# Opening of a two-layer decoder trunk: shift and scale columns of a chunk in one tile, TensorE in the first steps, even rates for the later vectors

## The chip, the cores and the metric

The kernel runs on one core of a Trainium2 chip. The metric is the device time of one execution in microseconds (us), lower is better; the time of a kernel is the median of its runs.

The engines that matter are TensorE (PE: matmuls and transposes; PEld: its weight loads), VectorE (DVE), ScalarE (ACT), GpSimd (POOL) and SyncE (SP), which issues most of the transfers. Each engine works through its own list of instructions in order; they wait for each other on semaphores.

## The reference

One sequence of 256 tokens, width 2048, goes through two layers. Each has a token mixer (layer 0: forgetting attention, `fox`; layer 1: sliding-window attention, `swa`) and a gated feed-forward block with a short convolution. Each of the four sub-layers is modulated by vectors that come from one conditioning vector `c`:

```python
c_act = silu(c)                                    # (1, 2048)
for i in range(2):
    mod = c_act @ ada_w[i] + ada_b[i]              # ada_w[i]: 2048 x 12288, float32
    sh1, sc1, g1, sh2, sc2, g2 = split(mod, 6)
    h = x * (1 + sc1) + sh1
    y = fox_attention(h, ...) if i == 0 else swa_attention(h, positions, ...)
    x = layer_norm(ALPHA * x + (1 + g1) * y, ln_mix_g[i], ln_mix_b[i])
    h = x * (1 + sc2) + sh2
    y = conv_ffn(h, ...)
    x = layer_norm(ALPHA * x + (1 + g2) * y, ln_ffn_g[i], ln_ffn_b[i])
```

All is float32. A vector (`sh1` and so on) is the product of a row of 2048 with a 2048 x 2048 block of `ada_w`, 16.8 MB that are read once.

## The kernel before

**Weights.** A weight tile is 256 rows by 512 columns (`[128, 2, 512]`, 512 KB). `stream` issues its transfer on SP, ACT copies it to the rounded half `wh`, DVE subtracts to get the low half `wl`, and PE multiplies with three products of halves: 24 matmuls of 256 columns where the weights are stationary (`w_mm`, results `ws`), 12 of 512 columns where the activations are (`x_mm`, results `xs`). The activations are kept as halves `hH`, `hL`, transposed, in 16 row chunks of 128. The pool `wp` has ten tile buffers for all tiles that SP loads, `hl` four pairs of halves. A planner in the framework orders the instructions of each engine; instructions given to `pin` keep their place in the program.

**Vectors.** `ada_vector(l, v)` makes vector v of layer l. It reads `ada_w` in 32 tiles (`wa`), and DVE adds each, scaled by an element of `cact`, to an accumulator `acc` of 128 x 2048 whose partitions still have to be summed. For a gate (v 2 and 5, a row) PE sums with `onep`. For a column vector four groups of four PE transposes of `acc` are summed by ACT, and `finish` makes the columns `cv`. A vector in `HELD`, (0,4) and (1,4), is not summed there: its PE sums (`sums`, 16 matmuls with `ones`) are kept in `held` until `release`, which `between` calls in the layer norm that needs it, and no later vector starts before. Each tile of weights that PE has used is a tick (`ada_tick`): it adds `ada["rate"]` to a debt, and each whole unit of it is one step of the running vector (usually one `wa` tile and one DVE product). `ada_need` runs steps until a vector is there.

**Opening.** The first products need the shift and scale of layer 0, v 0 and 1. `opening` makes them in five stages of 2, 2, 4, 4 and 4 column chunks (`widths`). In a stage `sums` loads the tiles of the shift and then those of the scale (`wo`); DVE does 14 of the 16 row chunks of each, PE chunks 7 and 15, as products with one column (`cps`). Then PE adds DVE's accumulator `oacc` with `ones`, DVE adds the bias (`cv`), and `mod_turn` (transposes of x) and `mod_pair` give the chunks of `hH` and `hL`. While a stage's vectors come in, PE works on weight tiles of the attention's input projection for the chunks that the earlier stages made (`plan`: 0, 3, 9, 12 and 12 tiles in the five stages, 6 more behind them).

**Later.** Then blocks 1, 2 and 3 of the projection (54 tiles) with the attention heads in between, `out_proj` (32 tiles, four quarters of the columns, the first two together), the layer norm with `between`, and the feed-forward block. The rates of the ticks are 0 in the opening, then 1.2 to 1.4, and in `out_proj` 1.4, 1.4 and 1.8 in the last two quarters.

**Layer norm.** `residual` adds the gated result to x, 512 columns at a time, and gathers statistics on DVE; POOL makes 1/sqrt (`rs`), `normalise` scales the first half of the tokens on ACT and the second on DVE, and `modulate` transposes, shifts and scales for the next sub-layer. `fox` clears `fh` and `fl`, the halves of the forget weights, with POOL.

Of the kernel before, what the change touches and what calls it, by code (L numbers as in the profile page):

```python
# [41 lines left out]
def hybrid_trunk(ctx: ExitStack, tc: tile.TileContext, a: dict, out: bass.AP):  # L42
# [31 lines left out]
    def mm(o, lhsT, rhs, start=False, stop=False, **kw):  # L74
        return nc.tensor.matmul(o, lhsT, rhs, start=start, stop=stop, **kw)  # L75
# [11 lines left out]
    def split_v(h, l, src):  # L87
        nc.vector.tensor_copy(h, src)
        nc.vector.tensor_tensor(l, src, f32(h), op=ALU.subtract)


    rows0 = ttile("rows0").rearrange("p (a b) -> p a b", b=P)
# [3 lines left out]
    nc.sync.dma_start(rows0[:NADA, 1, :], adab[0])  # L96

    ident = cst.tile([P, P], F32, name="ident")
    nc.gpsimd.memset(ident, 0.0)
    nc.gpsimd.affine_select(out=ident, in_=ident, compare_op=ALU.not_equal, fill=1.0, base=0,  # L100
                            pattern=[[-1, P]], channel_multiplier=1)
    ones = cst.tile([P, P], F32, name="ones")
    nc.gpsimd.memset(ones, 1.0)
    onep = cst.tile([P, P], F32, name="onep")
# [27 lines left out]
    nc.tensor.transpose(pt[:, :NADA], rows0[:NADA, 1, :], ident[:NADA, :NADA])  # L132
    nc.vector.tensor_copy(acol[:, 0, :], pt[:, :NADA])

    NF = 2 * DFF // P
# [228 lines left out]
    gates = {}  # L364
    ada_list = [(0, 2), (0, 3), (0, 4), (0, 5), (1, 0), (1, 1), (1, 3), (1, 2), (1, 4), (1, 5)]
    ada = {"gen": None, "debt": 0.0, "rate": 0.0, "gate_free": True}

    held = []
    HELD = {(0,4):False,(1,4):False}

# [144 lines left out]
    def opening(plan, proj, prep):  # L515
# [5 lines left out]

        def sums(c0, CB, v, acc, ps):
            QK = 1024 // CB
            nb = CB // P
            for kq in range(0, KC, QK):
                w = wp.tile([P, QK, CB], F32, tag="w", name="wo")
                nc.sync.dma_start(w, a["ada_w"][0, kq * P:(kq + QK) * P, v * D + c0:v * D + c0 + CB]
                                  .rearrange("(k p) f -> p k f", p=P))
                for k in range(QK):
                    kc = kq + k  # L530
                    if kc % 8 >= 8 - 1:
                        for j in range(nb):
                            c = nb * v + j
                            mm(ps[:, c:c + 1], w[:, k, j * P:(j + 1) * P], cact[:, kc:kc + 1],
                               start=c == 0 and kc == 8 - 1, skip_group_check=True)
                    elif kc == 0:
                        nc.vector.tensor_scalar_mul(acc[:, v, :], w[:, k, :], cact[:, kc:kc + 1])
                    else:
                        nc.vector.scalar_tensor_tensor(acc[:, v, :], w[:, k, :], cact[:, kc:kc + 1],
                                                       acc[:, v, :], op0=ALU.mult, op1=ALU.add)  # L540
                yield
# [3 lines left out]
        for s_, items in enumerate(plan):  # L545
            todo = [(*it, part) for it in items for part in range(3)]
            n = len(todo)
            if s_ == len(widths):
                for it in todo:
                    proj(*it)  # L550
                break
# [4 lines left out]
            ps = bank("cps")  # L556
            steps = [g for v in range(2) for g in [sums(c0, CB, v, acc, ps)] * (KC * CB // 1024)]
            for i, g in enumerate(steps):
# [6 lines left out]
            if s_ == 1:  # L565
                prep()
            for c in range(2 * nb):
                mm(ps[:, c:c + 1], acc[:, c // nb, c % nb * P:(c % nb + 1) * P], ones[:, 0:1],
                   stop=True, skip_group_check=True)
            for k in range(k0, k0 + nb, 2):  # L570
                tps = mod_turn(k)
                if k == k0:
                    for v in range(2):
                        nc.vector.scalar_tensor_tensor(cols[0, v][:, k:k + nb], ps[:, nb * v:nb * (v + 1)], float(v),
                                                       acol[:, 0, v * KC + k:v * KC + k + nb],
                                                       op0=ALU.add, op1=ALU.add)
                mod_pair(cols[0, 1], cols[0, 0], k, tps)

# [123 lines left out]
    def out_proj(oT, full, w_o, l):  # L702
# [11 lines left out]
        for i, ks in enumerate((range(0, 8), range(8, 12))):  # L714
            then(lambda i=i: ada.update(rate=((1.4,1.4,1.8,1.8), (0.85,)*4)[l][i]))
            for d in range(2):
                part(d, list(ks))
        then(lambda: ada_need(l, 2))
        for d in range(D // WB):
            if d < 2:  # L720
                part(d, list(range(12, KC)))
            else:
                then(lambda d=d: ada.update(rate=((1.4,1.4,1.8,1.8), (0.85,)*4)[l][d]))
                ps[d] = x_banks()
                part(d, list(range(KC)))
            then(lambda d=d: defer(residual(ps[d], d, gates[l, 2], True)), d == D // WB - 1)
# [3 lines left out]
    def fox(l, j):  # L730
# [7 lines left out]
        for q in range(4):  # L738
            nc.gpsimd.memset(f32(fh[q]), 0.0)
            nc.gpsimd.memset(f32(fl[q]), 0.0)  # L740

# [148 lines left out]
        later([forget(), columns(), rotary(), scaled()])  # L890
        for blk, rate in zip((0, 1, 2, 3), (1.2, 1.2, 1.3, 1.4)):
            then(lambda rate=rate: ada.update(rate=rate))
# [249 lines left out]
```

## Time and profile before

| | |
|---|---|
| median of 3 runs | 2278.0 us (2277.01 to 2279.0) |
| profiled execution | 2279.87 us, its span 2278.0 us |
| mean granted clock of TensorE | 0.985 |
| busy: PE, DVE, ACT, POOL | 2217.5, 1800.6, 1159.0, 26.6 us |
| read from memory | 598.37 MB, 264 GB/s over the span |

The profile is that of one execution. A row of a timeline has the start, the time, the engine, the line, the operation, what it writes and reads with their shapes, the count (x), and in brackets the idle time of the engine before it with what ended it. A row of a table by stretches has the stretch, its length, the busy time of PE, PE's weight loads, DVE, ACT and POOL (with counts), the granted clock as a share of full speed, the share of the transfer engines and GB/s. A row of waits says who waited for whom, the microseconds in total, how often, and the longest.

### The profile page before, as it was taken

To read this page: it belongs to the slowest core of one execution; us is meant where nothing else is said; L and a number is where in the kernel's file an instruction comes from. 1 tells how busy PE (TensorE), PEld (TensorE's weight loads), DVE (VectorE), ACT (ScalarE), POOL (GpSimd) and SP (SyncE) were. 2 spreads that over 40 slices of the span, in tenths; PEclk is the share of its full clock that TensorE was granted. 3 is DMA by queue.
4 is the path that set the end of the run, shared out by engine and by line. 5 is a ranking of instruction groups with operands and counts; after the bars stand their busy time and mean duration, and the time that the engine had idled before them with its cause. 6 is when DMAs were issued, how large, how long until landed. Compare 5 with 4: busy or idle time off the path is not lost. (4 is left out here: it accounts for less than half of the span.)

```text
span 2278.0 us, 38425 instructions
## 1 busy us (share of the span) xinstructions
PE 2217.5 (97%) x14933; PEld 2037.1 (89%) x14933; DVE 1800.6 (79%) x2509; ACT 1159.0 (51%) x1821; POOL 26.6 (1%) x61
## 2 busy tenths in 40 slices
PE   5999999999999999999999999999999999999997
PEld 5899998789999988999987788789999988999986
DVE  7877988979969978789788888779878555566656
ACT  2435565445555543555644588745555533454532
POOL 1001000000000000000000000000000000000000
PEclk8999999989999999999999999999999999999999
DMA  9998989879978989889888676658878556666563
GB/s 335 340 337 278 351 303 373 310 268 318 326 257 303 309 274 350 277 277 312 276 303 299 222 268 215 215 181 291 264 259 267 185 193 193 188 189 191 186 194 111
DMA packets 273720, 603.01 MB, mean 265 GB/s; under 512 B 20790, under 2 KB 29176, under 8 KB 273024
## 3 DMA queue, kind: packets, MB, share of 16 engines
q1 hardware_dynamic: 272480, 595.85, 77.1%
q0 software_dynamic: 1056, 4.69, 0.6%
q8 instruction: 117, 1.92, 0.3%
q14 instruction: 67, 0.55, 0.1%
HBM read 598.37 MB, written 2.10 MB: 264 GB/s over the span
## 5 line engine op out<-in xcount | busy, mean ns | idle before, releaser
L266 ACT CAST wh<-w 128x1024 fp32r<-128x1024 f32 x728 | 764.4, 1052 | 860.6 <-PE ws L75 319.9
L277 DVE TENSOR_TENSOR wl<-w,wh 128x1024 fp32r<-128x1024 f32 x728 | 888.9, 1222 | 376.4 <-ACT wh L266 358.0
L75 PE MATMUL ws<-hH,wh 128*128 128x256 f32 x3328 | 937.7, 282 | 10.5 <-ACT wh L266 10.5
L75 PE MATMUL ws<-hH,wl 128*128 128x256 f32 x3328 | 930.0, 281 | 4.3 <-DVE wl L277 4.3
L75 PE MATMUL ws<-hL,wh 128*128 128x256 f32 x3328 | 933.3, 281 | 0.2 <-DVE hL L85 0.2
L75 PEld LDWEIGHTS ws<-hH,wh 128*128 128x128 f32 x3328 | 629.9, 189 | 15.1 <-ACT wh L266 11.5
L75 PEld LDWEIGHTS ws<-hH,wl 128*128 128x128 f32 x3328 | 628.1, 189 | 5.4 <-DVE wl L277 5.2
L75 PEld LDWEIGHTS ws<-hL,wh 128*128 128x128 f32 x3328 | 630.4, 189 | 2.8 <-issue 1.9
L75 PE MATMUL xs<-wh,gT 128*128 128x512 f32 x1408 | 435.5, 389 | 0.0
L75 PEld LDWEIGHTS xs<-wh,gT 128*128 128x128 f32 x1408 | 264.3, 188 | 54.8
L75 PE MATMUL xs<-wl,gT 128*128 128x512 f32 x704 | 273.9, 389 | 0.0
L395 DVE SCALAR_TENSOR_TENSOR acc<-wa,cact,acc 128x1024 f32<-128x1024 f32 x180 | 228.4, 1278 | 0.0
L395 DVE SCALAR_TENSOR_TENSOR acc<-wa,cactp,acc 128x1024 f32<-128x1024 f32 x128 | 162.7, 1279 | 0.0
L75 PEld LDWEIGHTS xs<-wl,gT 128*128 128x128 f32 x704 | 132.2, 188 | 27.2
L75 PE MATMUL xs<-wh,hH 128*128 128x512 f32 x352 | 143.6, 414 | 0.3 <-ACT hH L492 0.3
L75 PE MATMUL xs<-wl,hH 128*128 128x512 f32 x352 | 141.7, 403 | 0.0
L75 PE MATMUL xs<-wh,hL 128*128 128x512 f32 x352 | 139.8, 400 | 0.0
L75 PE MATMUL xs<-wh,oT 128*128 128x512 f32 x384 | 127.7, 402 | 0.9 <-ACT pT L687 0.8
L1029 ACT ACTIVATE u<-ws,ccol 128x256 f32<-128x256 f32 x176 | 96.6, 561 | 56.4 <-PE ws L75 47.0
L1030 DVE SCALAR_TENSOR_TENSOR u<-ws,ccol,u 128x255 f32<-128x255 f32 x176 | 82.7, 478 | 19.9 <-ACT u L1029 19.8
L75 PEld LDWEIGHTS xs<-wh,oT 128*128 128x128 f32 x384 | 73.5, 192 | 16.4 <-ACT pT L687 1.2
L1032 DVE SCALAR_TENSOR_TENSOR u<-ws,ccol,u 128x254 f32<-128x254 f32 x176 | 83.4, 478 | 2.1
(219 smaller groups left out, 1615.1 us busy)
## 6 DMA issues: line engine op xcount, KB each, us to landing
w<-in_ffn_w_up_dram SPq DMA_DIRECT2D x352, 512.0 KB, 4.7
wa<-in_ada_w_dram SPq DMA_DIRECT2D x320, 512.0 KB, 5.5
w<-in_ffn_w_down_dram SPq DMA_DIRECT2D x176, 512.0 KB, 4.8
w<-in_fox_w_in_dram SPq DMA_DIRECT2D x96, 512.0 KB, 6.5
wo<-in_ada_w_dram SPq DMA_DIRECT2D x64, 512.0 KB, 8.7
w<-in_swa_w_in_dram SPq DMA_DIRECT2D x40, 512.0 KB, 5.1
w<-in_fox_w_o_dram SPq DMA_DIRECT2D x32, 512.0 KB, 7.0
w<-in_swa_w_o_dram SPq DMA_DIRECT2D x32, 512.0 KB, 4.9
```

The lines of the kernel that those rows point to most:

```text
L75: return nc.tensor.matmul(o, lhsT, rhs, start=start, stop=stop, **kw)
L266: pin(nc.scalar.copy(h, w), False)
L277: pin(nc.vector.tensor_tensor(l, w, f32(h), op=ALU.subtract), behind[0] > 0)
L395: pin(nc.vector.scalar_tensor_tensor(ac, wo, (cactp if row else cact)[:, k:k + 1], ac, op0=ALU.mult, op1=ALU.add), True)
L1029: nc.scalar.activation(u, pf, AF.Identity, bias=cw(CW, f), scale=cw(2, f))
L1030: nc.vector.scalar_tensor_tensor(u[:, 1:], pf[:, :S - 1], cw(1, f), u[:, 1:], op0=ALU.mult, op1=ALU.add)
L1032: nc.vector.scalar_tensor_tensor(u[:, 2:], pf[:, :S - 2], cw(0, f), u[:, 2:], op0=ALU.mult, op1=ALU.add)
```

## The change

- `opening` loads shift and scale columns of a chunk together: one tile has two row chunks (stages 0 and 1) or one (the others), and both vectors' columns beside each other, `[128, QK, 2, CB]`; each row chunk is a transfer of its own. So DVE's step covers both vectors. Per stage, 16 steps less those that PE does.
- PE does the odd row chunks in stage 0, chunks 3, 7, 11 and 15 in stage 1, and chunk 15 alone in the others (`onpe`). The totals of DVE's accumulator stand ahead of the last chunk's products.
- `busy(n)` runs n float32 matmuls of `ones` with `ones` that nobody reads: 4 and 5 at the start, 3 behind each of PE's row chunks in stage 0.
- The first stage's transposes go to two banks and its modulation uses the form that writes `hH` straight from ACT.
- `HELD` is empty: (0,4) and (1,4) are summed by transposes and ACT like the others, and later vectors may start at once.
- The first two vectors change places. The rate is 1.32 from the opening's last weight tiles through all of layer 0's attention, 0.6 in the last quarter of `out_proj`; in layer 1 the last quarter has 0.3 instead of 0.85.
- `fh` and `fl` are cleared by ACT instead of POOL; `ones` is filled ahead of `ident`.

```diff
@@ -88,6 +88,12 @@
         nc.vector.tensor_copy(h, src)
         nc.vector.tensor_tensor(l, src, f32(h), op=ALU.subtract)
 
+    def busy(n):
+
+        o = bank("idle")
+        for _ in range(n):
+            mm(o[:, :P], ones, ones, start=True, stop=True)
+
 
     rows0 = ttile("rows0").rearrange("p (a b) -> p a b", b=P)
     NADA = 6 * KC
@@ -95,12 +101,13 @@
     adab = a["ada_b"].rearrange("l (r p) -> l r p", p=P)
     nc.sync.dma_start(rows0[:NADA, 1, :], adab[0])
 
+    ones = cst.tile([P, P], F32, name="ones")
+    nc.gpsimd.memset(ones, 1.0)
+    busy(4)
     ident = cst.tile([P, P], F32, name="ident")
     nc.gpsimd.memset(ident, 0.0)
     nc.gpsimd.affine_select(out=ident, in_=ident, compare_op=ALU.not_equal, fill=1.0, base=0,
                             pattern=[[-1, P]], channel_multiplier=1)
-    ones = cst.tile([P, P], F32, name="ones")
-    nc.gpsimd.memset(ones, 1.0)
     onep = cst.tile([P, P], F32, name="onep")
     nc.gpsimd.memset(onep, 1.0 / P)
 
@@ -131,6 +138,7 @@
     pt = bank()
     nc.tensor.transpose(pt[:, :NADA], rows0[:NADA, 1, :], ident[:NADA, :NADA])
     nc.vector.tensor_copy(acol[:, 0, :], pt[:, :NADA])
+    busy(5)
 
     NF = 2 * DFF // P
     HR = ROPE_DIM // 2
@@ -362,11 +370,11 @@
 
     cols = {}
     gates = {}
-    ada_list = [(0, 2), (0, 3), (0, 4), (0, 5), (1, 0), (1, 1), (1, 3), (1, 2), (1, 4), (1, 5)]
+    ada_list = [(0, 3), (0, 2), (0, 4), (0, 5), (1, 0), (1, 1), (1, 3), (1, 2), (1, 4), (1, 5)]
     ada = {"gen": None, "debt": 0.0, "rate": 0.0, "gate_free": True}
 
     held = []
-    HELD = {(0,4):False,(1,4):False}
+    HELD = {}
 
     def ada_vector(l, v):
         row = v % 3 == 2
@@ -519,25 +527,43 @@
         for v in range(2):
             cols[0, v] = cst.tile([P, KC], F32, tag=f"cv{v}", name="cv")
 
-        def sums(c0, CB, v, acc, ps):
-            QK = 1024 // CB
+
+        onpe = [range(1, KC, 2), range(3, KC, 4)] + [(KC - 1,)] * 3
+
+        def products(w, c0, CB, kc, ps, first):
             nb = CB // P
+            for c in range(2 * nb):
+                mm(ps[:, c:c + 1], w[:, c // nb, c % nb * P:(c % nb + 1) * P], cact[:, kc:kc + 1],
+                   start=c == 0 and first, stop=kc == KC - 1, skip_group_check=True)
+
+        def totals(CB, acc, ps, first):
+            nb = CB // P
+            for c in range(2 * nb):
+                mm(ps[:, c:c + 1], acc[:, c // nb, c % nb * P:(c % nb + 1) * P], ones[:, 0:1],
+                   start=c == 0 and first, skip_group_check=True)
+
+        def sums(s_, c0, CB, acc, ps):
+            QK = 512 // CB
+            pe = onpe[s_]
             for kq in range(0, KC, QK):
-                w = wp.tile([P, QK, CB], F32, tag="w", name="wo")
-                nc.sync.dma_start(w, a["ada_w"][0, kq * P:(kq + QK) * P, v * D + c0:v * D + c0 + CB]
-                                  .rearrange("(k p) f -> p k f", p=P))
+                w = wp.tile([P, QK, 2, CB], F32, tag="w", name="wo")
+                for k in range(QK):
+                    nc.sync.dma_start(w[:, k], a["ada_w"][0, (kq + k) * P:(kq + k + 1) * P, :2 * D]
+                                      .rearrange("p (v f) -> p v f", f=D)[:, :, c0:c0 + CB])
                 for k in range(QK):
                     kc = kq + k
-                    if kc % 8 >= 8 - 1:
-                        for j in range(nb):
-                            c = nb * v + j
-                            mm(ps[:, c:c + 1], w[:, k, j * P:(j + 1) * P], cact[:, kc:kc + 1],
-                               start=c == 0 and kc == 8 - 1, skip_group_check=True)
-                    elif kc == 0:
-                        nc.vector.tensor_scalar_mul(acc[:, v, :], w[:, k, :], cact[:, kc:kc + 1])
-                    else:
-                        nc.vector.scalar_tensor_tensor(acc[:, v, :], w[:, k, :], cact[:, kc:kc + 1],
-                                                       acc[:, v, :], op0=ALU.mult, op1=ALU.add)
+                    if kc not in pe:
+                        if kc == 0:
+                            nc.vector.tensor_scalar_mul(acc, w[:, k], cact[:, kc:kc + 1])
+                        else:
+                            nc.vector.scalar_tensor_tensor(acc, w[:, k], cact[:, kc:kc + 1], acc,
+                                                           op0=ALU.mult, op1=ALU.add)
+                        continue
+                    if kc == KC - 1:
+                        totals(CB, acc, ps, len(pe) == 1)
+                    products(w[:, k], c0, CB, kc, ps, kc == pe[0] and len(pe) > 1)
+                    if s_ == 0:
+                        busy(3)
                 yield
 
         accs = cst.tile([P, D], F32, tag="acc", name="oacc").rearrange("p (c v f) -> p c v f", c=2, v=2)
@@ -546,6 +572,7 @@
             todo = [(*it, part) for it in items for part in range(3)]
             n = len(todo)
             if s_ == len(widths):
+                then(lambda: ada.update(rate=1.32))
                 for it in todo:
                     proj(*it)
                 break
@@ -554,7 +581,7 @@
             pair += widths[s_]
             acc = accs[:, s_ % 2, :, :CB]
             ps = bank("cps")
-            steps = [g for v in range(2) for g in [sums(c0, CB, v, acc, ps)] * (KC * CB // 1024)]
+            steps = [sums(s_, c0, CB, acc, ps)] * (KC * CB // 512)
             for i, g in enumerate(steps):
                 if i == len(steps) // 2 and c0 % 512 == 0:
                     c = slice(c0, c0 + 512)
@@ -564,17 +591,14 @@
                     proj(*todo.pop(0))
             if s_ == 1:
                 prep()
-            for c in range(2 * nb):
-                mm(ps[:, c:c + 1], acc[:, c // nb, c % nb * P:(c % nb + 1) * P], ones[:, 0:1],
-                   stop=True, skip_group_check=True)
             for k in range(k0, k0 + nb, 2):
-                tps = mod_turn(k)
+                tps = mod_turn(k, 2 if k == 0 else 1)
                 if k == k0:
                     for v in range(2):
                         nc.vector.scalar_tensor_tensor(cols[0, v][:, k:k + nb], ps[:, nb * v:nb * (v + 1)], float(v),
                                                        acol[:, 0, v * KC + k:v * KC + k + nb],
                                                        op0=ALU.add, op1=ALU.add)
-                mod_pair(cols[0, 1], cols[0, 0], k, tps)
+                mod_pair(cols[0, 1], cols[0, 0], k, tps, k == 0)
 
 
     stats = cst.tile([P, NT, D // 512, nc.vector.BN_STATS_DIM], F32, name="stats")
@@ -712,7 +736,7 @@
             stream(w_o, 0, d * WB, ks, use)
 
         for i, ks in enumerate((range(0, 8), range(8, 12))):
-            then(lambda i=i: ada.update(rate=((1.4,1.4,1.8,1.8), (0.85,)*4)[l][i]))
+            then(lambda i=i: ada.update(rate=((1.32, 1.32, 1.32, 0.6), (0.85, 0.85, 0.85, 0.3))[l][i]))
             for d in range(2):
                 part(d, list(ks))
         then(lambda: ada_need(l, 2))
@@ -720,7 +744,7 @@
             if d < 2:
                 part(d, list(range(12, KC)))
             else:
-                then(lambda d=d: ada.update(rate=((1.4,1.4,1.8,1.8), (0.85,)*4)[l][d]))
+                then(lambda d=d: ada.update(rate=((1.32, 1.32, 1.32, 0.6), (0.85, 0.85, 0.85, 0.3))[l][d]))
                 ps[d] = x_banks()
                 part(d, list(range(KC)))
             then(lambda d=d: defer(residual(ps[d], d, gates[l, 2], True)), d == D // WB - 1)
@@ -736,8 +760,8 @@
         fh, fl = ([gtile(n).rearrange("p a b -> p (a b)").rearrange("p (k f) -> p k f", f=P) for _ in range(4)]
                   for n in ("fh", "fl"))
         for q in range(4):
-            nc.gpsimd.memset(f32(fh[q]), 0.0)
-            nc.gpsimd.memset(f32(fl[q]), 0.0)
+            for f in (fh[q], fl[q]):
+                nc.scalar.mul(f, ones.rearrange("p (o f) -> p o f", o=1).broadcast_to([P, 4, P]), 0.0)
 
         def prep():
             for b in range(4):
@@ -888,7 +912,7 @@
         opening(plan, first_block, prep)
         settle()
         later([forget(), columns(), rotary(), scaled()])
-        for blk, rate in zip((0, 1, 2, 3), (1.2, 1.2, 1.3, 1.4)):
+        for blk, rate in zip((0, 1, 2, 3), (1.32,) * 4):
             then(lambda rate=rate: ada.update(rate=rate))
             q, k, V = [], [], []
             n = done.get(blk, 0)
```

## The prediction

> **What bounds the kernel now.** I read the page first, then the busy time by stretches of 57 us, then TensorE's waits, then the timelines of the two places where they fall.
>
> ```profile
> span 2278.0 us, 38425 instructions
> ...
> PE 2217.5 (97%) x14933; PEld 2037.1 (89%) x14933; DVE 1800.6 (79%) x2509; ACT 1159.0 (51%) x1821; POOL 26.6 (1%) x61
> ```
>
> TensorE (PE) is the bound: 2278.0 - 2217.5 leaves 60.5 us idle. Its work on the weights is not touched by the change. What can be won is idle time and time at half clock; both lie in few places:
>
> ```profile
> 0.00:57.00 57.00, 32.57 (x164) 29.70 (x164) 43.17 (x88) 12.95 (x19) 8.06 (x30) 0.88 1.03 335
> 57.00:114.00 57.00, 52.73 (x350) 48.56 (x349) 46.30 (x60) 24.23 (x32) 0.00 (x0) 0.92 0.97 340
> ...
> 399.00:456.00 57.00, 53.18 (x237) 43.09 (x236) 52.93 (x69) 24.34 (x45) 0.00 (x0) 0.94 0.89 311
> 456.00:513.00 57.00, 52.41 (x284) 45.88 (x284) 45.49 (x64) 24.70 (x31) 1.74 (x3) 0.88 0.72 265
> ```
>
> The columns are length, busy time of PE, its weight loads, DVE, ACT and POOL, granted clock, DMA share, GB/s. The first two rows (the opening) lack 28.7 us of PE, the last two (out-projection of layer 0 and the layer norm behind it) 8.4 us, and the clock is below 1 in all four. Who is late:
>
> ```profile
> PE cps L75 <- DMA wo<-in_ada_w_dram: 10.9, 5, 3.6
> PE ws L75 <- ACT wh L266: 10.5, 4, 3.9
> PE xs L75 <- DVE wl L277: 7.2, 3, 3.5
> PE ws L75 <- DVE wl L277: 4.3, 4, 2.5
> ```
>
> The first, second and fourth are the opening, the third is the out-projection. In the opening VectorE (DVE) and the transfers press together, and PE's clock falls when it waits; in the out-projection DVE is alone. The four rows are the stretches that the sums below use:
>
> ```profile
> 10.00:20.00 10.00, 4.94 (x20) 4.28 (x20) 8.42 (x22) 0.00 (x0) 0.00 (x0) 1.00 1.08 349
> ...
> 40.00:50.00 10.00, 5.29 (x20) 4.71 (x21) 9.79 (x17) 3.19 (x6) 0.00 (x0) 0.50 1.04 384
> ...
> 450.00:460.00 10.00, 9.94 (x31) 7.93 (x32) 10.00 (x10) 3.15 (x3) 0.00 (x0) 0.69 1.00 378
> ...
> 470.00:480.00 10.00, 6.98 (x24) 5.59 (x25) 8.20 (x8) 2.85 (x4) 0.00 (x0) 0.83 1.05 389
> ```
>
> **The opening, DVE's and PE's work.** The five ends of stages in the old kernel are the `cv` rows; the first two rows below price DVE's product steps:
>
> ```profile
> 23.44 0.23 DVE L574 SCALAR_TENSOR_TENSOR cv<-cps,acol 128x2 f32<-128x2 f32 x2 [0.71 <-PE cps L75]
> ...
> 28.65 4.29 DVE L539 SCALAR_TENSOR_TENSOR oacc<-wo,cact,oacc 128x256 f32<-128x256 f32 x10
> ...
> 38.65 0.22 DVE L574 SCALAR_TENSOR_TENSOR cv<-cps,acol 128x2 f32<-128x2 f32 x2
> ...
> 49.17 3.10 DVE L539 SCALAR_TENSOR_TENSOR oacc<-wo,cact,oacc 128x512 f32<-128x512 f32 x4
> ...
> 81.56 0.23 DVE L574 SCALAR_TENSOR_TENSOR cv<-cps,acol 128x4 f32<-128x4 f32 x2 [1.94 <-PE cps L75]
> ...
> 128.49 0.23 DVE L574 SCALAR_TENSOR_TENSOR cv<-cps,acol 128x4 f32<-128x4 f32 x2 [5.96 <-PE cps L75]
> ...
> 171.03 0.23 DVE L574 SCALAR_TENSOR_TENSOR cv<-cps,acol 128x4 f32<-128x4 f32 x2 [4.82 <-PE cps L75]
> ```
>
> A 256-wide step costs 0.43 us, a 512-wide one 0.78. For a 1024-wide one, and for DVE's low half of a weight tile (`wl`), the out-projection has rows, beside the longest wait there:
>
> ```profile
> 444.01 4.85 DVE L395 SCALAR_TENSOR_TENSOR acc<-wa,cact,acc 128x1024 f32<-128x1024 f32 x4
> 473.49 3.48 DVE L277 TENSOR_TENSOR wl<-w,wh 128x1024 fp32r<-128x1024 f32 x3
> 450.06 0.80 PE L75 MATMUL xs<-wl,oT 128*128 128x512 f32 x1 [3.50 <-DVE wl L277]
> ```
>
> So 1.21 us a step and 1.16 a `wl`. Stages 0 and 1: 56 x 0.43 = 24.1 before; after, 8 and 12 steps of 512, 20 x 0.78 = 15.6: DVE saves 8.5. Stages 2 to 4: 28 x 0.78 = 21.8 each before, 15 x 1.21 = 18.2 after: 3.6 each. DVE is relieved of 19 us in all.
>
> PE's price for a product or a total depends on its clock:
>
> ```profile
> 11.23 1.12 PE L482 MATMUL sm<-ident,x 128*128 128x128 f32 x4 [0.29 <-DMA x<-in_x_dram]
> ...
> 17.60 1.01 PE L75 MATMUL cps<-cact,wo 128*128 128x1 f32 x4 [1.99 <-DMA wo<-in_ada_w_dram]
> ...
> 26.69 0.58 PE L75 MATMUL ws<-hH,wh 128*128 128x256 f32 x1 [3.29 <-ACT wh L266]
> ...
> 32.40 0.41 PE L75 MATMUL ws<-hL,wh 128*128 128x256 f32 x1
> 32.62 0.41 PE L75 MATMUL ws<-hH,wl 128*128 128x256 f32 x1
> ...
> 33.00 0.28 PE L75 MATMUL ws<-hL,wh 128*128 128x256 f32 x1
> 33.12 0.28 PE L75 MATMUL ws<-hH,wl 128*128 128x256 f32 x1
> ...
> 70.86 0.95 PE L75 MATMUL cps<-cact,wo 128*128 128x1 f32 x8
> ```
>
> One float32 matmul stands as two pieces: 0.25 us a piece cold, 0.12 warm. Matmuls of 256 columns start 0.22 apart until 32.62 and 0.12 from 33.00: the clock doubled some 6.3 us after the dense work began (26.69). A weight tile of 24 such matmuls is 2.8 us warm. Stages 2 to 4 lose 8 matmuls of `cps` each: 16 x 0.12 = 1.9 us of PE saved per stage. Stage 0 gains 24: per pair of row chunks now 4 products (8 pieces) and 3 fillers (6 pieces). The fillers, 128 columns on `ones`, have no row; nearest are the transposes (1.12 / 4 = 0.28 cold) and the products (0.12 warm): 0.7 to 1.7 us for three. A pair is thus 0.95 + 0.7 = 1.7 us warm, 2.0 + 1.7 = 3.7 cold, while the transfer of its 0.52 MB at 349 GB/s takes 1.5. PE becomes the pace of stage 0.
>
> When is it warm? Its fillers start near 1 us but wait for the conditioning vector, which ScalarE now reaches after two of the eight moved fills and a second table load (no cover; up to 3 us, and I take it to be ready near 5, where the first weights land anyway). Dense from 5, warm at 5 + 6.3 = 11. From 5 on: two transposes and five cold fillers, 3.4; one cold pair, 3.7; six warm ones, 10.2; then transposes of x, totals and the last products, 8 pieces each, about 2. That makes 24 for the first `cv` (23.44 before); bounds 21 (warm from 5 on) and 40 (never warm: 8.4 + 7 x 3.7 + 5).
>
> The Trainium skill ("TensorE: Matmul & The Clock Gate", Part 1) says that one busy window of about 3.4 us opens the clock. By it PE would be warm at 8.4, the cold pair would go, and the first `cv` would be 2 us earlier. I used the trace's 6.3 us.
>
> **The opening, stage by stage.** Stage 1 on DVE: modulation, four passes of 256 columns at about 0.5, then 12 x 0.78 and two `wl` 2.3: 13.7; totals and products 1.9: 24 + 15.6 = 39.6 (38.65 before). But its three weight tiles are then done near 43 with the clock up; before, PE stood and then ran at 0.50 in 40 to 50. Stage 2 on DVE: modulation and forget-weight halves, passes of 256 and 512 columns, 2.9; nine `wl` 10.4; 15 steps 18.2; then totals and products 32 pieces x 0.12 = 3.8: 35.3, so 74.9. Its transfers (45 tiles of 0.52 MB up to there, 23.6 MB, at about 365 GB/s, from 3 us) land by 68 and allow it. I take 76 (81.56 before). Stages 3 and 4: DVE 12 x 1.16 + 18.2 + modulation 2.4 = 34.5; totals, products and ten weight matmuls between them 5: 39.5. PE's own sum is no longer: 12 x 2.8 + 3.8. By the same sum the old ones are 21.8 + 13.9 + 2.4 + 4 = 42.1 and took 46.9 and 42.5, 2.6 above on average; so 42.1 each now. The last `cv` is at 76 + 84 = 160 against 171.0: **-11 us**. The next place where weights are late is the out-projection (third wait row), so this is kept if DVE still leads in between. There ten vector steps more run by the end of block 1 (6 x 1.32 in the opening's last stage, 18 x 0.12 behind it), 12.1 us of DVE, against 19 saved ahead of them. Bounds: -20 and +13.
>
> **The out-projection.** Before, 1.8 vector steps ride on each weight tile of its last columns: 1.8 x 1.21 + 1.16 = 3.3 us of DVE a tile, now 1.32 x 1.21 + 1.16 = 2.8, and in the last quarter none is left: 84 tiles at 1.32 make 110.9 steps, and the last product is step 109 (38 + 39 + 32). PE lost 7.2 idle, and at clock 0.69 and 0.83 another 3.1 + 1.7 us: 12 in all. In the built orders 12 steps stand between the first and the third residual, before 17, and the longest clump is 3 steps, not 4: 6 us of DVE less. The wait in the last quarter (about half) goes, the one at 450 shrinks: **-8 us**, bounds -12 and -2. What is late next there is DVE's residual work, which stays.
>
> **The layer norms.** Two vectors were summed behind the last product; the layer norm inside the feed-forward, which has no such sums, is the comparison:
>
> ```profile
> 488.07 4.77 PE L75 MATMUL sm<-ones,acc 128*128 128x1 f32 x32
> ...
> 496.11 0.80 PE L75 MATMUL ws<-hH,wh 128*128 128x256 f32 x2
> ...
> 1242.81 0.39 PE L75 MATMUL xs<-wh,gT 128*128 128x512 f32 x1
> ...
> 1248.12 0.80 PE L75 MATMUL xs<-wh,hH 128*128 128x512 f32 x1 [0.33 <-ACT hH L492]
> ...
> 1253.82 0.93 PE L482 MATMUL sm<-ident,x 128*128 128x128 f32 x7
> ...
> 1516.31 3.63 PE L75 MATMUL sm<-ones,acc 128*128 128x1 f32 x32
> ...
> 1523.17 0.79 PE L75 MATMUL ws<-hH,wh 128*128 128x256 f32 x2
> ```
>
> From the last product's end to the first new one: 8.0 and 6.9 us with the sums, 5.1 without (about 1243.0 to 1248.1). That wins 2.9 + 1.8 = 4.7. In their place 32 transposes run among the products, where PE is the bound: 32 x 0.93 / 7 = 4.3 us. ScalarE's 32 sums beside them have cover (2.85 to 3.15 of 10 busy). POOL's bias row for the next vector is ahead of both `rs` in the built order, waiting for transposes done a quarter earlier: nothing. Sum **-0.5**, bounds -4.7 and +4.3. The lower rates in layer 1 cost nothing: its vectors are needed long after.
>
> **Sum.** -11 - 8 - 0.5 = -19.5. The profiled execution took 2279.87 us (span 2278.0): 2260.4; the median of the runs, 2278.0, is 1.9 lower: **2258.5 us**.
>
> **The rivals.** (1) *Stage 0 stays cold* (ends slower). If loads with one-column products do not hold the clock, the first `cv` is at 40, the ten tile buffers stand full, stage 1 ends at 40 + 13.7 + 4 = 58, stage 2 at 58 + 37 = 95, 13.5 after the old; with the old pace of the later stages that stays, less 8.5 from the other places: 2283. For it: clock 0.50 in 40 to 50 though PE was busy half of it. Against: fillers are near half of each pair. It decides from a first `cv` past 35.
>
> (2) *DVE gives it back.* The ten earlier steps and the earlier PE meet where DVE is already full, before the third block ends; the 11 us return as waits for `wl`: 2278 - 8.5 = 2269.5.
>
> (3) *Halved transfers.* The loads of stages 0 and 1 are 256 KB now, and each issue waits for the landing of the eighth before it.
>
> ```profile
> wo<-in_ada_w_dram SPq DMA_DIRECT2D x29, 512.0 KB, 9.2
> ```
>
> If landing still took 9.2 us, eight halves in flight would give 2.1 MB / 9.2 us = 228 GB/s, and the 10 MB of two stages 44 us instead of 28.6: 15 lost of the 11 won, so 2278 + 4 - 8.5 = 2273.5. Against: 9.2 us is mostly queueing, which halves too. The Trainium skill ("DMA: Bandwidth & Descriptors", the cost of one DMA) puts about 2 us of fixed cost on each transfer, which speaks for this rival; a queue of eight hides it as long as it holds.
>
> (4) *All stalls of the opening go*, stages at 39 us and no cold stretch: -25 there, 2244.5.
>
> **How the numbers follow.** Forecast 0.62 (its own range 2247 to 2269), (1) 0.10, (2) 0.13, (3) 0.08, (4) 0.07. The range 2244 to 2275 takes in (2), (3) and (4) and the bounds of the terms. A measurement of this kernel tells about 0.2%, 4.6 us: faster than 2273.4 has 0.6 from the forecast, 0.07 from (4), most of (2), little of (3): 0.79. Within: 0.12. Slower: 0.09, from (1).
>
> **What would show it.** The `cv` rows near 24, 40, 76, 118 and 160; products at 0.12 a piece from 12 us on; no PE wait of 3 us for `wl` in the out-projection; 5 us between products at both attention layer norms. First `cv` past 35, DMA below 250 GB/s in 10 to 30, or PE waits for `wl` between 180 and 300 would make it wrong.

## The result, and the profile after

The changed kernel took **2283.4 us** (median of 11 runs, 2278.8 to 2286.7) against 2277.0 for the old one on the same chip: ratio 1.0029, 95% interval 1.0020 to 1.0038. It is slower by about 6.6 us; the forecast was 2258.5. Its profiled execution took 2283.28 us (span 2281.5), 3.4 more than that of the old kernel.

The page's head, and four rows of the table by stretches of 57 us (columns as before):

```profile
span 2281.5 us, 38538 instructions
...
PE 2232.5 (98%) x14983; PEld 2050.5 (90%) x14983; DVE 1787.0 (78%) x2436; ACT 1174.0 (51%) x1894; POOL 23.4 (1%) x53
```

```profile
0.00:57.00 57.00, 49.66 (x225) 48.20 (x226) 19.65 (x35) 12.38 (x18) 4.59 (x22) 1.00 0.79 253
57.00:114.00 57.00, 52.14 (x320) 46.78 (x320) 47.21 (x49) 22.19 (x31) 0.00 (x0) 0.94 0.97 329
...
171.00:228.00 57.00, 56.14 (x430) 52.73 (x429) 47.77 (x57) 28.32 (x35) 4.75 (x10) 1.00 1.00 356
228.00:285.00 57.00, 56.29 (x401) 52.06 (x400) 54.32 (x91) 36.69 (x86) 0.24 (x1) 1.00 0.95 334
```

PE is busy 17 us more in the first stretch (49.66, before 32.57), yet DVE does half (19.65, before 43.17) and the transfers run at 253 GB/s instead of 335. PE became the pace of the opening's first stage, at half clock. The clock column prints 1.00 there only because the trace holds no clock record before 62.4 us; the starts of the matmuls tell. PE's timeline at the head, and where the clock rises:

```profile
1.00 2.08 PE L75 MATMUL idle<-ones 128*128 128x128 f32 x8 [1.00 <-POOL ones L105]
4.95 0.26 PE L133 MATMUL sm<-ident,csil 16*128 16x16 f32 x1 [1.87 <-ACT csil L130]
...
7.53 1.71 PE L75 MATMUL cps<-cact,wo 128*128 128x1 f32 x8
9.10 1.63 PE L75 MATMUL idle<-ones 128*128 128x128 f32 x6
10.52 1.71 PE L75 MATMUL cps<-cact,wo 128*128 128x1 f32 x8
...
28.30 1.63 PE L75 MATMUL idle<-ones 128*128 128x128 f32 x6
...
61.91 0.63 PE L75 MATMUL xs<-wh,hL 128*128 128x512 f32 x1
62.34 0.44 PE L75 MATMUL xs<-wl,hH 128*128 128x512 f32 x1
62.62 0.39 PE L75 MATMUL xs<-wh,hL 128*128 128x512 f32 x1
```

Row chunk by row chunk, 8 pieces of products and 6 of fillers repeat every 2.99 us (7.53, 10.52), without a gap and without the clock rising: 0.2 us a piece to the end. Only at 62.3, in the first long run of wide products, do starts go from 0.43 to 0.23 apart. The stage ends (DVE's timeline, waits for PE's `cps` in brackets):

```profile
34.02 0.23 DVE L598 SCALAR_TENSOR_TENSOR cv<-cps,acol 128x2 f32<-128x2 f32 x2 [13.72 <-PE cps L75]
...
56.40 0.23 DVE L598 SCALAR_TENSOR_TENSOR cv<-cps,acol 128x2 f32<-128x2 f32 x2 [4.28 <-PE cps L75]
...
96.18 0.23 DVE L598 SCALAR_TENSOR_TENSOR cv<-cps,acol 128x4 f32<-128x4 f32 x2 [4.93 <-PE cps L75]
...
139.64 0.23 DVE L598 SCALAR_TENSOR_TENSOR cv<-cps,acol 128x4 f32<-128x4 f32 x2 [5.47 <-PE cps L75]
...
180.90 0.23 DVE L598 SCALAR_TENSOR_TENSOR cv<-cps,acol 128x4 f32<-128x4 f32 x2 [3.56 <-PE cps L75]
```

10.6 us behind at the first (23.44 before), 9.9 at the last (171.03). PE's waits show the later parts doing their work:

```profile
PE qp L1002 <- ACT pT L711: 3.7, 2, 1.9
...
PE xs L75 <- DVE wl L285: 2.4, 2, 1.8
```

`xs` waits 2.4 us for `wl`, before 7.2; the wait for `pT` in layer 1's attention has grown from 1.4 to 3.7.

### The profile page after: what moved, and what is told of

Its sections match the earlier page's. It is cut to its first block, busy times and chain, and to the rows that moved or that the text cites. A ratio compares the mean times of both kernels' runs of the same rounds, so it can differ in the third digit from the quotient of the medians.

```text
span 2281.5 us, 38538 instructions
## 1 busy us (share of the span) xinstructions
PE 2232.5 (98%) x14983; PEld 2050.5 (90%) x14983; DVE 1787.0 (78%) x2436; ACT 1174.0 (51%) x1894; POOL 23.4 (1%) x53
## 5 line engine op out<-in xcount | busy, mean ns | idle before, releaser
L1053 ACT ACTIVATE u<-ws,ccol 128x256 f32<-128x256 f32 x176 | 96.4, 561 | 55.6 <-PE ws L75 48.8
```

The lines of the kernel that those rows point to most:

```text
L1053: nc.scalar.activation(u, pf, AF.Identity, bias=cw(CW, f), scale=cw(2, f))
```

## The experiments

Each was timed beside the old kernel on the same chip, and its ratio is to that. Theory A: stage 0 given to a cold PE costs the opening 10 us, and the fillers are its larger part.

**Fillers left out.** `busy` returns at once:

```diff
     def busy(n):
-        o = bank("idle")
-        for _ in range(n):
-            mm(o[:, :P], ones, ones, start=True, stop=True)
+        return
```

> Edit: the 33 filler matmuls on the tile of ones are left out of the changed kernel; its output is the same. Theory A (a TensorE that never leaves half clock is the pace of stage 0): a pair of row chunks costs 8 pieces of 0.2 us instead of 14 of 0.21, so 7 or 8 pairs shed about 1.3 us each and the head 2; first cv falls from 34.0 to 24 or 25, fourth and fifth cv by 8 to 10; time 8 to 10 us under the changed kernel, ratio to the old one 0.998 to 0.9995. Theory B (halved transfers or the merged tiles pace stage 0): first cv stays at 31 or later, ratio stays near 1.003. Theory C (the fillers do hold the clock up to some degree): clock or cv rows get worse, ratio above 1.003.

2272.6 us, ratio 0.9972 (0.9961 to 0.9983). The 33 fillers cost 0.57% of the time, 13 us (1.0029 to 0.9972; the profiled spans differ by 12.5). DVE's timeline:

```profile
23.08 0.23 DVE L596 SCALAR_TENSOR_TENSOR cv<-cps,acol 128x2 f32<-128x2 f32 x2 [4.16 <-PE cps L75]
...
45.46 0.23 DVE L596 SCALAR_TENSOR_TENSOR cv<-cps,acol 128x2 f32<-128x2 f32 x2 [4.28 <-PE cps L75]
...
83.87 0.23 DVE L596 SCALAR_TENSOR_TENSOR cv<-cps,acol 128x4 f32<-128x4 f32 x2 [3.56 <-PE cps L75]
...
125.77 0.23 DVE L596 SCALAR_TENSOR_TENSOR cv<-cps,acol 128x4 f32<-128x4 f32 x2 [3.91 <-PE cps L75]
...
167.62 0.23 DVE L596 SCALAR_TENSOR_TENSOR cv<-cps,acol 128x4 f32<-128x4 f32 x2 [3.65 <-PE cps L75]
```

Theory A holds for the first row; the gain was larger than expected because every later row moved with it, by 11 to 14 us. Halved transfers are no cause: they are still there. Without them the first row is 0.4 us ahead of the old kernel's 23.44, so the fillers were the whole loss of stage 0; with products alone on a cold PE the stage is no later than the old one. But the opening so mended ends only 3.4 us ahead of the old one, not the 11 that were forecast.

**All vector sums on DVE.** No fillers, and:

```diff
-        onpe = [range(1, KC, 2), range(3, KC, 4)] + [(KC - 1,)] * 3
+        onpe = [(KC - 1,)] * 5
```

> Edit: no fillers, and TensorE takes only the last row chunk in every stage of the opening, so stages 0 and 1 have their products on VectorE as 512-wide steps over the merged tiles; the later parts of the change stay. Theory A: stage 0 is paced by transfers and 15 steps of 0.78 us, first cv at 19 to 23, second at 36 to 40, third at 71 to 76; the opening ends 9 to 15 us earlier than in the changed kernel, time 2264 to 2271, ratio 0.994 to 0.998. Theory B (merged tiles and halved transfers are the cost): first cv at 28 or later, ratio 1.000 or above.

2276.1 us, 0.9993 (0.9984 to 1.0001): theory A's range was missed. The rows came at 25.6, 43.4, 85.8, 127.8 and 171.1. DVE was last in stage 0 (PE's totals waited for its accumulator until 22.0); in its queue a step on the sink row, whose small transfer landed at 12.4, held the products behind it:

```profile
12.46 0.18 DVE L185 TENSOR_SCALAR nsink<-sink 128x32 f32<-128x32 f32 x1 [3.22 <-DMA sink<-in_swa_sinks_dram]
```

Stage 1 was quick (17.8 us), but stage 2 took 42.4 and gave it back. PE's timeline shows the clock rise 3.2 us after the wide products begin (43.25), though PE had been busy with float32 pieces since 39.81:

```profile
39.81 1.86 PE L75 MATMUL cps<-ones,oacc 128*128 128x1 f32 x8 [13.27 <-DVE oacc L557]
41.54 1.84 PE L75 MATMUL cps<-cact,wo 128*128 128x1 f32 x8
43.25 0.56 PE L75 MATMUL ws<-hH,wh 128*128 128x256 f32 x1
...
46.17 0.41 PE L75 MATMUL ws<-hL,wh 128*128 128x256 f32 x1
46.38 0.32 PE L75 MATMUL ws<-hH,wl 128*128 128x256 f32 x1
46.53 0.28 PE L75 MATMUL ws<-hH,wh 128*128 128x256 f32 x1
```

**The opening alone**, the later parts as before:

```diff
-    HELD = {}
+    HELD = {(0,4):False,(1,4):False}
...
-            then(lambda i=i: ada.update(rate=((1.32, 1.32, 1.32, 0.6), (0.85, 0.85, 0.85, 0.3))[l][i]))
+            then(lambda i=i: ada.update(rate=((1.4,1.4,1.8,1.8), (0.85,)*4)[l][i]))
...
-        for blk, rate in zip((0, 1, 2, 3), (1.32,) * 4):
+        for blk, rate in zip((0, 1, 2, 3), (1.2, 1.2, 1.3, 1.4)):
```

> Edit: the opening of the changed kernel (with its fillers, and the fills on ScalarE) together with the old later parts: old rates, old order of the vectors, sums behind the layer norms' last product. Theory A: the opening keeps its cv rows (34, 56, 96, 140, 181) and the loss of 10 us at the end of the opening is carried to the end, the later gains of 6 are missing: 2285 to 2289, ratio 1.004 to 1.006. Rival (later parts cost, the opening's loss is made up in stalls that shrink): below the changed kernel, ratio under 1.002.

2285.4 us, 1.0037 (1.0024 to 1.0051): +8.4 us, at the edge of theory A's range; its seven runs spread from 2284 to 2295. The first rows were the same, 34.0 and 56.4, the last at 182.1. The rival is out.

**The later parts alone:** the reverse edit on the old kernel, with the rate of 1.32 from the opening's last tiles on.

> Edit: the old opening with the later parts of the change alone (even rate of 1.32 from the opening's last stage on, 0.6 and 0.3 in the last quarter, both vectors summed ahead of the layer norms). Theory A: as the changed kernel's trace has it, out-projection -3.7, layer norms -2.9 and -1.6, sliding-window attention of layer 1 +3.9, the rest about -1: 2272 to 2275, ratio 0.997 to 0.9985. Rival (later parts are worth the 8.5 that was forecast): ratio 0.9963 or below. Rival (even rate costs more than it wins): 1.000 or above, with waits for wl between 180 and 400.

2271.3 us, 0.9964 (0.9952 to 0.9976): -8.2 us, the size that was forecast (-8.5), at the rival's edge; the intervals hold both. On the late opening the same parts brought 1.0037 to 1.0029; these two intervals overlap, so whether they are worth less there isn't settled. Its time and that of the changed kernel without fillers can't be told apart either: new or old opening, without fillers, is the same to the measurement.

**Which work holds the clock?** Three kernels with other fillers, rounded-float matmuls on a tile of ones that lies in `hH`. First, 12 of 512 columns at the head and none later; second, two more of them behind the products of each row chunk in stage 0; third, the fillers of the change in number and shape, but of rounded type (two for each float32 one). The edit of the first; the second has `busy(2)` behind the products, the third `busy(8)`, `busy(10)` and `busy(6)` of 128 columns:

```diff
+    hH = cst.tile([P, KC, S], F32R, name="hH")
+    dense = hH[:, KC - 2:, :].rearrange("p a s -> p (a s)")
+    nc.vector.memset(f32(dense), 1.0)
...
-            mm(o[:, :P], ones, ones, start=True, stop=True)
+            mm(o, dense[:, :P], dense, start=True, stop=True)
...
-    busy(4)
+    busy(12)
...
-    busy(5)
-                    if s_ == 0:
-                        busy(3)
```

> Edit: the fillers of the changed kernel go; instead 12 rounded-float matmuls of 512 columns run at the head, ahead of the transpose of the conditioning vector, and none behind it. Theory D (the clock follows how much streams through the array: wide matmuls open it, short float32 ones neither open nor hold it): the clock opens near 5 to 7 us and falls again within 7 us of the first products; first cv at 20 to 23, the later rows at or up to 3 us ahead of those without fillers (23.1, 45.5, 83.9, 125.8, 167.6); time within 4 us of 2272.6. Rival (only idle time closes the clock, products hold it): products at 0.12 a piece from 7 us on, first cv at 18 to 20, second at 34 to 38, last at 160; 2263 to 2267.

2286.1 us, 1.0034 (1.0021 to 1.0047). PE's timeline:

```profile
1.46 5.41 PE L75 MATMUL idle<-hH 128*128 128x512 f32 x12 [1.46 <-DVE hH L93]
...
7.29 1.05 PE L75 MATMUL cps<-cact,wo 128*128 128x1 f32 x8
8.82 1.05 PE L75 MATMUL cps<-cact,wo 128*128 128x1 f32 x8 [0.47 <-DMA wo<-in_ada_w_dram]
10.28 3.57 PE L75 MATMUL cps<-cact,wo 128*128 128x1 f32 x16 [0.41 <-DMA wo<-in_ada_w_dram]
...
14.83 5.28 PE L75 MATMUL cps<-cact,wo 128*128 128x1 f32 x24
```

The wide matmuls open the clock (products at 0.13 a piece from 7.29), and after one stretch of about 3.4 us, with products and 0.9 us of waiting, it is shut again (0.21 a piece from 10.28). As theory D had it for the clock; the rows of `cv`, 23.6 to 169.3, are within 2.5 us of those without fillers. The time, 13 us more, was not expected; most of it is lost past 490 us (below, the moved tile).

> Edit: as the run with 12 wide matmuls at the head, and two more of them (512 columns, rounded float) behind the products of each row chunk that TensorE takes in stage 0, in place of three float32 fillers of 128 columns. Theory D: with a third or more of the time in wide matmuls the clock stays open; a pair of chunks costs 0.95 + 4 x 0.23 = 1.9 us warm, first cv at 20 to 23, second at 36 to 39, last at 158 to 163; 2264 to 2269. Rival (short float32 products close the clock whatever lies between): a pair costs 1.9 + 1.7 = 3.6 us, first cv at 35 or later, 2283 or more.

2287.9 us, 1.0048 (1.0034 to 1.0062). Neither way: the clock went up and down with what the stretch was made of.

```profile
10.37 1.70 PE L75 MATMUL cps<-cact,wo 128*128 128x1 f32 x8
11.93 1.20 PE L75 MATMUL idle<-hH 128*128 128x512 f32 x2
12.93 1.70 PE L75 MATMUL cps<-cact,wo 128*128 128x1 f32 x8
14.49 3.87 PE L75 MATMUL idle<-hH 128*128 128x512 f32 x10
...
18.63 3.15 PE L75 MATMUL cps<-cact,wo 128*128 128x1 f32 x24
21.64 1.84 PE L75 MATMUL cps<-ones,oacc 128*128 128x1 f32 x8
```

Two wide ones between eight pieces (about 40% of the time) leave it shut; ten in a row open it (24 products in 3.15 us), and it shuts again by 21, though PE had no gap from 14.49 on. First `cv` 25.2, last 169.4.

> Edit: the changed kernel with each float32 filler (two pieces of 128 columns) replaced by two rounded-float matmuls of the same 128x128 shape; number of pieces and places unchanged. If the type of the fillers is what the clock does not count: clock open by 15 us, a pair at 1.7 us, first cv near 24, time 2262 to 2270. If the number of columns or the one-column products between them are the reason: clock closed until 60, first cv at 33 to 35, time within 3 us of the changed kernel (2283).

2291.5 us, 1.0057 (1.0045 to 1.0069); first `cv` at 31.9, the clock shut until 47.5. So the float32 type is not what keeps the clock shut: rounded fillers of 128 columns did no more. What opens it is wide matmuls, 256 or 512 columns, through most of a stretch.

**The moved tile.** These three had `hH` allocated first. The kernel without fillers, with that line moved and nothing else:

> Edit: no fillers, and the tile hH is allocated ahead of the constants instead of behind the rotary tables; not one instruction is changed, only where tiles lie. The three runs with other fillers had hH there, and their feed-forwards ran 6.8 us longer each (matmuls of 256 columns at 281 to 283 ns instead of 279 to 281). If the place of the tile does that: 12 to 15 us more than without fillers, 2284 to 2288, cv rows as without fillers. If the fillers of those runs did it: 2272 to 2274.

2288.5 us, 1.0038 (1.0025 to 1.0051): 0.66%, 15 us, from where tiles lie (`hH`, and with it those allocated between its two places). In the grouped rows of 600 to 1200 us, first without fillers, then with the tile moved, the matmuls themselves are slower; the three unmoved kernels that were timed on the same chip as the moved one have 281 too:

```profile
L75 PE MATMUL ws<-hH,wh 128*128 128x256 f32 x1095 | 307.7, 281 | 0.0
```

```profile
L75 PE MATMUL ws<-hH,wh 128*128 128x256 f32 x1107 | 313.1, 283 | 0.0
```

So the three runs above are read for their openings alone; their times hold this too.

**What binds stages 3 and 4?** Without fillers they took 41.9 us each, close to the forecast 42.1 of which VectorE and PE were said to make 39.5. The table by stretches, stage 2 and these two without fillers:

```profile
45.50:83.90 38.40, 33.49 (x212) 29.42 (x213) 31.14 (x33) 13.74 (x20) 0.00 (x0) 1.00 1.00 351
83.90:125.80 41.90, 38.36 (x274) 34.94 (x274) 34.10 (x34) 18.56 (x23) 0.00 (x0) 1.00 1.02 361
125.80:167.60 41.80, 39.51 (x281) 35.91 (x280) 34.42 (x33) 15.36 (x17) 2.52 (x5) 1.00 1.01 359
```

PE and DVE have some room, the transfers none: 41.9 x 361 makes 15.1 MB, what a stage reads. Two kernels relieve one side each in these stages, without fillers: the first loads only every second row chunk and computes the next from the same tile, the second loads all and cuts DVE's odd steps to 64 columns.

```diff
+                if s_ < 3 or kq % 2 == 0:
+                    w = wp.tile([P, QK, 2, CB], F32, tag="w", name="wo")
...
+                            n = CB // 16 if s_ > 2 and kc % 2 else CB
```

> Edit: no fillers, and in stages 3 and 4 of the opening only every second row chunk of the modulation weights is loaded; the chunk behind it is computed from the same tile again, so all steps and products stay and 4.2 MB of 15 are not transferred in each stage (the output is not the reference's). Theory F (transfers set these stages: about 15 MB at 366 to 387 GB/s is 39 to 41.5 us, and they take 41.9): each of the two falls below 40, to the sum of VectorE and TensorE, 37 to 39.5; last cv at 158 to 163 instead of 167.6; time 3 to 8 us under 2272.6 as far as no later place eats it. Rival G (VectorE's sum of 39.5 and its waits set them): 41 to 42 each, time as without fillers.

> Edit: no fillers, and in stages 3 and 4 the vector steps of the odd row chunks (7 each stage) cover 64 instead of 1024 columns; every load stays (the output is not the reference's). VectorE is relieved of about 7 x 1.1 = 7.5 us a stage. Theory F (transfers): stages stay at 40.5 to 42, last cv at 165 to 168, time within 2 us of 2272.6. Rival G (VectorE): stages at 34 to 37, last cv at 153 to 158.

2267.5 us (0.9951, 0.9939 to 0.9964) and 2271.2 (0.9966, 0.9952 to 0.9979). The last three stage ends of the one and of the other:

```profile
84.54 0.23 DVE L597 SCALAR_TENSOR_TENSOR cv<-cps,acol 128x4 f32<-128x4 f32 x2 [3.56 <-PE cps L75]
...
122.50 0.23 DVE L597 SCALAR_TENSOR_TENSOR cv<-cps,acol 128x4 f32<-128x4 f32 x2 [2.70 <-PE cps L75]
...
161.01 0.23 DVE L597 SCALAR_TENSOR_TENSOR cv<-cps,acol 128x4 f32<-128x4 f32 x2 [1.82 <-PE cps L75]
```

```profile
84.03 0.23 DVE L597 SCALAR_TENSOR_TENSOR cv<-cps,acol 128x4 f32<-128x4 f32 x2 [3.67 <-PE cps L75]
...
127.06 0.23 DVE L597 SCALAR_TENSOR_TENSOR cv<-cps,acol 128x4 f32<-128x4 f32 x2 [7.47 <-PE cps L75]
...
168.73 0.23 DVE L597 SCALAR_TENSOR_TENSOR cv<-cps,acol 128x4 f32<-128x4 f32 x2 [4.69 <-PE cps L75]
```

Half the loads: 38.0 and 38.5 us. Seven of fifteen vector steps all but gone: 43.0 and 41.7. Theory F holds for the size: transfers bind, and relieving DVE there is worth nothing. But what is next is not the sum of DVE and PE, as theory F had put it; with half the loads gone it is PE, which in the last stage is busy all the time:

```profile
84.50:122.50 38.00, 36.37 (x261) 33.64 (x261) 34.00 (x34) 19.07 (x24) 0.00 (x0) 1.00 0.92 311
122.50:161.00 38.50, 38.50 (x271) 36.32 (x271) 34.94 (x34) 16.49 (x18) 2.51 (x5) 0.96 0.90 290
```

The run with short vector steps alone would not tell the two apart: its clock was 0.92 and 0.97 in these stages, and PE was busy 95% and 97% of them.

**Stage 1 off TensorE.** No fillers, `onpe` for stage 1 is its last chunk:

```diff
-        onpe = [range(1, KC, 2), range(3, KC, 4)] + [(KC - 1,)] * 3
+        onpe = [range(1, KC, 2)] + [(KC - 1,)] * 4
```

> Edit: no fillers, and TensorE keeps only the last row chunk in stage 1 (stage 0 still gives it every second one). With every chunk but the last on VectorE in both, stage 1 took 17.8 us against 22.4. If a cold TensorE paces stage 1: second cv near 41, last cv at 163 to 165, time 2268 to 2270. If transfers decide from stage 2 on: second cv near 41 but third within 2 us of 83.9, time 2271 to 2274.

2275.0 us, 0.9983 (0.9973 to 0.9992): no gain. Second `cv` at 43.3, third at 87.1: stage 1 was 3 us quicker, stage 2 lost 5. Nearer to the second expectation, but the third row is 3.2 us late, which that doesn't explain; the transfer engines were full there too (share 0.99), but at 334 GB/s over 43.8 us, 14.6 MB, where it had been 351 over 38.4, 13.5 MB. So the load left over by a shorter stage 1 was moved in stage 2; why the rate fell stays open.

**Vector 4 of layer 1 summed behind the last product again**, without fillers:

```diff
-    HELD = {}
+    HELD = {(1,4):False}
```

> Edit: no fillers, and vector 4 of layer 1 is summed behind the last product of layer 1's out-projection again, as in the old kernel, instead of by transposes and ScalarE ahead of it. Theory E (ScalarE's sums delay the softmax of the sliding-window attention: TensorE's wait for pT grew from 1.4 to 3.7 us there): that wait returns to about 1.4, 2 to 4 us won between 1240 and 1510, 1.8 lost at the layer norm; 2270 to 2272.5. Rival (the loss there comes from when the steps run, not from the sums): the wait stays, time 1 to 2 us above the kernel without fillers (2274).

2272.6 us, 0.9976 (0.9966 to 0.9985), as without it. `qp` still waits 3.6 us for `pT`: theory E falls. From the first product of layer 1's attention to its last, 270.9 us instead of 272.2 (the 16 transposes are gone), and the layer norm behind it 6.7 instead of 5.1. The wait belongs to the later parts (3.6 us with them alone, 1.4 with the opening alone); what in them delays `pT` wasn't found.

## Why the prediction was wrong

**The step that failed** is "warm at 5 + 6.3 = 11" in the opening. The trace showed how long wide products had run until the clock doubled; I carried that time over to one-column products and 128-column fillers, as if any gapless work counted. It does not: PE ran without a gap from 5 to 35 us and the clock stayed shut until 62.4. So "one cold pair, six warm ones" became pairs at 2.99 us throughout (the cold price of 3.7 was itself too high: the 14 pieces took 0.21 each on average, not 0.25 to 0.28), and the first `cv` came at 34.0 instead of 24. Of the three signs that were to make the forecast wrong none came: 34.0 is not past 35, the transfers had 342 to 348 GB/s between 10 and 30, and PE doesn't wait for `wl` between 180 and 300.

The Trainium skill ("TensorE: Matmul & The Clock Gate", Part 1) gives a window of about 3.4 us that runs freely, and one busy window as the condition. The length agrees: the clock records of the changed kernel's trace last 3.41 us or a multiple of it (30.72, 6.83, 23.89). So how long wide products must run depends on where in a window they begin: 3.2 us from 43.25 in the run with all sums on DVE, where counting back from the first record a window began at 43.0; 6.1 us, from 56.22 to 62.34, in the changed kernel, where windows began at 55.6 and 59.0 and only the second, all wide, opened the clock. The forecast's 6.3 was one such case. What counts as busy is the other half: windows filled with short matmuls left the clock shut in every one of these runs.

**Rival (1), "stage 0 stays cold",** is what happened: it said 40, 58 and 95 for the first three ends and 2283 us; they were 34.0, 56.4, 96.2 and 2283.4. It had a chance of 0.10 because "fillers are near half of each pair"; the row that spoke for it (clock 0.50 in 40 to 50 with PE busy half of it) should have weighed more, and no row of the trace showed one-column work at full clock outside runs of wide products. That its 2283 is the measured time to the microsecond is luck: it kept 13.5 us of loss and won 8.5 behind it; the last row is 9.9 late, and the kernel 6.6 slower.

**The second mis-sized term** is the -11 itself. Without fillers the first end came at 23.1 and the last at 167.6, not 160. That the first is near the forecast 24 is luck: a warm pair with fillers was priced at 1.7 us, and a cold one without them took the same 1.7. The sum was made of DVE's and PE's work, and stages 3 and 4 came out right in size (42.1, measured 41.9) for the wrong reason: the transfers set them, and DVE relieved further bought nothing (what its first 3.6 us a stage bought against the old kernel, no run separates). Stages 1 and 2, forecast 16 and 36 us, took 22.4 and 38.4: in stage 1 PE was still cold and the transfers full too (share 1.03 at 316 GB/s), and stage 2 moved its bytes at 351 GB/s with the transfer engines full. I had let the first 23.6 MB land at 365 GB/s; over the first 57 us it was 298. The row before had said it: 1.03 and 0.97 of the transfer engines in the opening's two stretches.

**Rival (2)** didn't come either: neither with the fillers nor without them does PE wait for `wl` between 180 and 300 us. **Rival (3), halved transfers,** didn't come: the 256 KB loads landed in 6.0 us in the middle instead of 9.2 (not quite half, 4.6), and 10 to 30 us had 342 to 348 GB/s with fillers, 348 to 360 without.

**The later parts were right in size:** -8.5 forecast, -8.2 measured by themselves on the old opening (interval -10.9 to -5.5); on the late opening they brought 1.8 us, with the wider doubt said above. In detail: the gaps between products at the two attention layer norms are 4.9 and 5.1 us (5.1 forecast). In the out-projection of the changed kernel the longest wait for `wl` is 1.8 us, and the two stretches that had clock 0.69 and 0.83 have 1.00; one shut window of 3.4 us is left, at 461.8, of 10.2 us before. From the first forget logit to the last product there:

```profile
L75 PE MATMUL lg<-hH,fh x16: 277/279/281, 205.2 to 212.8; 128*128 128x256 f32 x16
...
493.88 0.40 PE L75 MATMUL xs<-wh,hL 128*128 128x512 f32 x1
```

289.1 us, before 292.7 (195.5 to 488.2): 3.6 won, after 16 transposes (2.2 us, booked with the layer norms) and new holes of 0.6 us up to 285 (PE busy 79.09 of 79.80 us from 205.2 on, before 79.43 of 79.50 from 195.5) were paid; that makes 6.4, so -8 was some 1.6 us too much. "The lower rates in layer 1 cost nothing" missed 2.3 us: the wait for `pT`, which the summing there doesn't cause. It comes with the later parts; whether the rates cause it, no run shows.

## What to carry to other kernels

Don't put work on TensorE in a stretch without wide matmuls and count on full clock: price it at half clock, and don't add narrow fillers, which only lengthen the queue. Before relieving an engine, look up the transfer share of that very stretch: where it was 1.0 here, engine time saved became waiting time. A forecast borrowed from one kind of instruction (how long until the clock doubles) holds for that kind alone.

## What the runs showed of the hardware

- In these runs the clock followed how wide the matmuls were, not how busy PE was, in stretches of about 3.4 us: 100% busy PE in 10 to 30 us with products of 1 column and fillers of 128, of either type, stayed at half rate; ten matmuls of 512 columns in 3.87 us opened it, and gapless products from 18.63 closed it by 21.
- Where tiles lie can cost: `hH` allocated elsewhere, all instructions the same, raised the mean of the 256-column matmuls from 281 to 283 ns and the time by 0.66%. Which of the tiles that moved with it matters wasn't tried.
- Full transfer engines are not one rate: without fillers, at a share of 1.00 to 1.03 of the 16 engines, stage 1 moved 316 GB/s, stage 2 351, and stages 3 and 4 361 and 359.
